# Taking turns at the start: two column groups of the first projection alternate, and the first loads are ordered anew

## The chip, the core and the metric

The kernel runs on one core of a Trainium2 chip. The core has five engines with programs of their own: TensorE (PE: matrix products and transposes into PSUM), VectorE (DVE), ScalarE (ACT), GpSimd (POOL) and SyncE (SP, which here only issues DMA transfers). SP, ACT and POOL can issue DMAs, each on a queue of its own. The metric is the time of one execution on the device, in microseconds (us).

## What is computed

One layer of a hybrid decoder trunk, on 256 prompt tokens and on 32 sample tokens (8 sequences of 4) at once, in float32:

```
proj = x @ w_in                                # 2048 -> 11280 columns
gB, gC, h, q, k, v, z, b, a, m_a, m_b = split(proj)
y_a = (gB * conv3(gC * h)) @ w_a_out           # histories of the sample: state_conv_a
q, k, v = split(silu(conv4([q, k, v])))        # histories of the sample: state_gdn_conv
y_b = gated_norm(delta_rule(l2norm(q), l2norm(k), v, g(a), sigmoid(b), S0), z) @ w_b_out
x = LN(ALPHA * x + (sigmoid(m_a) * y_a + sigmoid(m_b) * y_b) @ w_o)
x = LN(ALPHA * x + relu(x @ w_up)**2 @ w_down)
```

The results are the outputs for both sets of tokens and the new histories and states.

## The kernel before

**Stream.** All large products form one stream of 496 blocks. A block is 512 rows by 256 columns of a weight matrix (512 KB, four chunks of 128 rows); a column group of `w_in` is four blocks, which add into one accumulator in PSUM (`acc`, two buffers). Features lie on the partitions, tokens along the row, so x has to be there feature-major: `xh`, `xl`, 16 tiles of 288 tokens (256 prompt, 32 sample). Float32 products are made of three products of a faster type: x and weights are each split into a high part (a rounded copy, made by ACT) and a low part (the difference, made by DVE), and `matmuls(i)` issues, for each of 4 chunks and 2 column halves, high x high (L202), high x low (L203) and low x high (L204): 24 products of 288 columns a block.

**Order.** The schedule is written out by hand; each engine does its instructions in the order in which the program issues them. The loop over i does `split_hi(i + 3)` (L177), one step of the side work, `split_lo(i + 3)` (L140, a helper's line), the evacuations due at i, `matmuls(i)`, and `load(i + 7)` (L169, on SP). There are four buffers each for the raw weights, the high and the low part. `fill` is a list of small steps of which one is issued after every three products.

**Evacuation.** When a group of `w_in` is done, `conv_evac` takes its two halves out of PSUM in two steps one block apart (ACT copies with the histories in front, DVE does the width-4 convolution); a third step applies SiLU.

**Side work.** Gates and the delta rule (`gates`, `gdn`) are generators; one step is taken for every block from i = 4 on, and all must be over at block 112 (`mark["merge"]`).

**Start.** `warm` feeds 8 products into PSUM that are not used. SP then loads the identity (`cf`, first 128 columns), and in turn, four times: a quarter of x for the prompt (512 KB), a quarter for the sample (32 partitions), a weight block. POOL issues 16 transfers of histories and convolution weights (`hwr`, `har`). `x_tile(k)` turns one chunk of x: two transposes for the prompt (L736), one for the sample (L737), an ACT copy to `xh` and a DVE difference to `xl`. The first four chunks are turned ahead of block 0, the other twelve through `fill` in blocks 0 to 2. SP goes on with weight block 4, nine transfers of constants and small weights (L1263 to L1271), and blocks 5 and on. `hist_tiles` (L744 to L749) turns the histories at i = 4.

Of the kernel before, what the change touches and what calls it, by code (L numbers as in the profile page):

```python
# [9 lines left out]
F32 = mybir.dt.float32  # L10
F32R = mybir.dt.float32r
# [5 lines left out]
P = 128  # L17
D = 2048
NP_ = 256
NS = 32  # L20
NT = NP_ + NS
# [15 lines left out]

# [1 line left out]

# [64 lines left out]
def hybrid_kernel(ctx: ExitStack, tc: tile.TileContext, A):  # L104
# [15 lines left out]
    def nm(s):  # L120
        counter[0] += 1
        return f"{s}{counter[0]}"

    def gtile():
        n = nm("g")
        return gp.tile([P, 512], F32, tag="g", name=n)
# [12 lines left out]
    def tt(out, a, b, op):  # L139
        dve.tensor_tensor(out=out, in0=a, in1=b, op=op)  # L140
# [5 lines left out]

# [1 line left out]
    w_in = A["w_in"][0]  # L148
# [15 lines left out]
    def load(i):  # L164
        if i >= len(blocks):
            return
        gi, r0, k0, _, _ = blocks[i]
        t = wp.tile([P, KB, GW], F32, tag="raw", name=nm("raw"))
        sp.dma_start(t, gi["W"][r0:r0 + KB * P, gi["col0"]:gi["col0"] + GW]  # L169
                     .rearrange("(k p) c -> p k c", p=P))  # L170
        raw[i] = t

    def split_hi(i, step=KB):
        if i < len(blocks):
            his[i] = wp.tile([P, KB, GW], F32R, tag="hi", name=nm("hi"))
            for k in range(0, KB, step):
                act.copy(his[i][:, k:k + step], raw[i][:, k:k + step])  # L177
# [32 lines left out]

# [1 line left out]
    NE, NL = CF_AT["early"], CF_AT["late"]  # L212
# [30 lines left out]

# [1 line left out]
    gd = {}  # L245
# [3 lines left out]
    def conv_evac(sec, G, p):  # L249
# [37 lines left out]
        def last(ps):  # L287
            a1(ps)
            b1(ps)
        return [a0, b0, last]  # L290

    mark = {}
    for G in range(2):
        mark["kqv", G] = len(blocks)
        for sec, c0 in ((1, C_K), (0, C_Q), (2, C_V)):
            for p in range(2):
                add_group(w_in, c0 + 512 * G + GW * p, 0, KT, acts_x, conv_evac(sec, G, p))
        mark["kqv_end", G] = len(blocks)

    def h_evac(p):  # L300
# [319 lines left out]
    def final():  # L620
# [31 lines left out]

        # sample: four rows of the tile hold a token
        def moments():
# [46 lines left out]

# [1 line left out]
    tx_cm = tc.tile_pool(name="tx", bufs=1)  # L703
# [3 lines left out]
    wps = gtile()  # L707
    for _ in range(8):
        pe.matmul(wps, warm[:, 0:P], warm, start=True, stop=True)
    xr = [tx.tile([P, 3, 512], F32, name=f"xr{i}") for i in range(4)]  # L710
    xpr = A["x_prompt"][0].rearrange("(b p) f -> p b f", p=P)
    xsr = A["x_sample"].rearrange("b t f -> (b t) f")
    sp.dma_start(cf[:, 0:128], A["cf"][:, 0:128])
    for i in range(4):
        c = slice(512 * i, 512 * i + 512)
        sp.dma_start(xr[i][:, 0:2, :], xpr[:, :, c])
        sp.dma_start(xr[i][0:NS, 2, :], xsr[:, c])
        load(i)
    hwr = tx.tile([112, 768], F32, name="hwr")
    har = tx.tile([76, 256], F32, name="har")  # L720
    for g in range(4):
        c, c2 = slice(768 * g, 768 * g + 768), slice(256 * g, 256 * g + 256)
        gps.dma_start(hwr[28 * g:28 * g + 24, :], A["state_gdn_conv"][0].rearrange("b j c -> (b j) c")[:, c])
        gps.dma_start(hwr[28 * g + 24:28 * g + 28, :], A["gdn_conv_w"][0][:, c])
        gps.dma_start(har[19 * g:19 * g + 16, :], A["state_conv_a"][0].rearrange("b j c -> (b j) c")[:, c2])
        gps.dma_start(har[19 * g + 16:19 * g + 19, :], A["conv_a_w"][0][:, c2])
    lnr = tx.tile([33, P], F32, name="lnr")
    gps.memset(epsc[:, 0:1], LN_EPS)
    gps.memset(epsc[:, 1:2], NORM_EPS)
    gps.memset(epsc[:, 2:3], 1.28e-10)  # L730

    def x_tile(k):
        i, kk = k // 4, k % 4
        g = gtile()
        for b in range(2):
            pe.transpose(g[:, b * P:(b + 1) * P], xr[i][:, b, kk * P:(kk + 1) * P], ident)  # L736
        pe.transpose(g[:, NP_:NT], xr[i][0:NS, 2, kk * P:(kk + 1) * P], ident[0:NS, 0:NS])  # L737
        act.copy(xh[:, k, :], g[:, 0:NT])
        tt(xl[:, k, :], g[:, 0:NT], xh[:, k, :], SUB)

# [15 lines left out]

# [1 line left out]
    G_ = {}  # L758
# [90 lines left out]

# [1 line left out]
    def gdn(G):  # L851
# [126 lines left out]

        # sample: states times keys and queries, one sequence's columns at a time
        def states_of(hh):  # L980
# [8 lines left out]

        # inverse by doubling  # L990
        def pairs(out, a, b):
# [44 lines left out]
        def sample():  # L1036
            # sample: kernels of the short sequences
            sp1 = gtile()
# [101 lines left out]
        yield  # L1140
        # prompt: chunk by chunk
        S = T([P, 4, P], "E")
# [42 lines left out]
        while not done:  # L1185
            yield
        # gated norm (the norm of the queries folded in), to feature-major
        so = T([P, 9], "so")
# [28 lines left out]

# [1 line left out]
    def states():  # L1219
# [29 lines left out]

# [1 line left out]
    cur = [0]  # L1251
    aux = []
    his[0] = wp.tile([P, KB, GW], F32R, tag="hi", name=nm("hi"))
    los[0] = wp.tile([P, KB, GW], F32R, tag="lo", name=nm("lo"))
    t = raw.pop(0)
    for k in range(KB + 2):
        if k < KB:
            x_tile(k)
        if k > 1:
            act.copy(his[0][:, k - 2], t[:, k - 2])  # L1260
            tt(los[0][:, k - 2], t[:, k - 2], his[0][:, k - 2], SUB)
    load(4)
    sp.dma_start(cf[:, 128:], A["cf"][:, 128:NE])  # L1263
    sp.dma_start(cfe, A["cf"][:, NE:NL])
    sp.dma_start(ci, A["ci"])
    sp.dma_start(lnr[0:16, :], A["ln1_g"].rearrange("o (k p) -> (o k) p", p=P))
    sp.dma_start(lnr[16:32, :], A["ln1_b"].rearrange("o (k p) -> (o k) p", p=P))
    sp.dma_start(lnr[32:33, :], A["gdn_norm_w"])
    sp.dma_start(wbar, w_in[:, C_BA:C_BA + 16].rearrange("(k p) c -> p k c", p=P))
    sp.dma_start(arow[:, 0, :], A["a_log"].to_broadcast([P, 8]))  # L1270
    sp.dma_start(arow[:, 1, :], A["dt_bias"].to_broadcast([P, 8]))  # L1271
    for i in range(3):
        split_hi(i + 1, 2)
        split_lo(i + 1, 2)
        load(i + 5)
        fill.extend(lambda k=k: x_tile(k) for k in range(4 * i + 4, 4 * i + 8))
        matmuls(i)
    for i in range(4, AHEAD + 3):
        split_hi(i)
        split_lo(i)  # L1280
        load(i + 4)
    sgen = side()
    gcm = None
    for p in range(8):
        for n, f in enumerate(residual1(p)):
            at(mark["up"] + 6 + 4 * p + n, f)
    for i in range(3, len(blocks)):
        cur[0] = i
        split_hi(i + AHEAD)
        if i == 4:  # L1290
            hist_tiles()
            tx_cm.__exit__(None, None, None)
            gcm = tc.tile_pool(name="gdn", bufs=1)
            gpool = gcm.__enter__()
            gd["pool"] = gpool
            for G in range(2):
                gd["kq", G] = gpool.tile([P, 4, 4, 2, 64], F32, tag="kq", name=f"kq{G}", bufs=2)
                gd["kqs", G] = gpool.tile([P, 2, 4, 8, 4], F32, tag="kqs", name=f"kqs{G}", bufs=2)
                gd["v", G] = gpool.tile([P, 2, 4, 2, 64], F32, tag="vf", name=f"vf{G}")
                gd["vs", G] = gpool.tile([P, 4, 8, 4], F32, tag="vfs", name=f"vfs{G}")  # L1300
        if i > 3 and sgen:
            if i == mark["merge"]:
                for _ in sgen:
                    pass
                sgen = None
            else:
                next(sgen, None)
                if aux and next(aux[0], aux) is aux:
                    aux.pop(0)
            if i == mark["conv"] + 1:  # L1310
                gd["ao"] = ap_.tile([P, 2, H, NT], F32, tag="ao", name="ao")
# [25 lines left out]
        matmuls(i)  # L1337
        load(i + AHEAD + 4)
    for i in sorted(due):
        for f in due[i]:  # L1340
            f()
# [30 lines left out]
```

## Time and profile before

| | |
|---|---|
| time, median of 3 runs | 1725.30 us (1725.29 to 1725.32) |
| span of the profiled execution, first to last instruction | 1725.5 us |
| PE busy | 1701.8 us (99%) |
| DVE busy | 1026.3 us (59%) |
| ACT busy | 712.0 us (41%) |
| POOL busy | 123.7 us (7%) |
| DMA | 279.76 MB, 162 GB/s over the span |
| granted clock of TensorE, mean | 0.991 |

The profiled execution's time is its span; the times of the three runs were taken apart from it. A profile row of the timeline gives the start (us from the span's start), the duration, the engine, the line, the operation, output<-input, sizes, the number of instructions, and in brackets how long the engine had been idle and what ended that. A row of windows gives a stretch and the busy time of each engine in it (number of instructions in brackets), then the granted clock of TensorE (1.00 is full speed), the share of time in which the DMA engines were busy, and GB/s. SPq is SP's issuing of DMAs; a row of DMA issues gives the number, the size and the us from issue to landing.

### The profile page before, as it was taken

The page shows a single profiled execution, that of the slowest core. Times are in us where ns is not written, and L with a number is a line of the kernel's source. Part 1 is how long each engine was busy: PE and PEld are TensorE (multiplying, and loading weights), DVE is VectorE, ACT ScalarE, POOL GpSimd, SP SyncE. Part 2 cuts the span into 40 slices and gives each one's busy share as a digit, 9 for nine tenths or more (in the row PEclk, how much of TensorE's full clock was granted, in tenths as well). Part 3 has the DMA queues.
Part 4 walks back from the last instruction along what each step waited for, and adds up shares of the span by engine and source line. Part 5 has one row for each costly group of instructions (what it writes and reads, how often), then busy time and mean ns, then how long its engine had stood idle before and what let it go on. Part 6 is the DMA issues. An engine that isn't in the chain of part 4 may idle for free.

```text
span 1725.5 us, 31070 instructions
## 1 busy us (share of the span) xinstructions
PE 1701.8 (99%) x13037; PEld 1677.6 (97%) x13037; DVE 1026.3 (59%) x1345; ACT 712.0 (41%) x1031; POOL 123.7 (7%) x217
## 2 busy tenths in 40 slices
PE   9999999999999999999999999999999999999997
PEld 7999889999999999999999999999999999999996
DVE  5687777577454445545778754565445654456565
ACT  4664445334443333434445433344333433344331
POOL 2221231023300000000010000000000000000000
PEclk8999999999999999999999999999999999999998
DMA  8464347435655555555575555555555555555552
GB/s 241 141 181 137 106 118 233 131 103 151 207 169 162 169 165 166 159 171 160 170 204 164 166 168 163 168 160 167 166 167 163 159 171 166 165 164 166 163 158 78
DMA packets 272296, 279.76 MB, mean 162 GB/s; under 512 B 12122, under 2 KB 267035, under 8 KB 272023
## 3 DMA queue, kind: packets, MB, share of 16 engines
q1 hardware_dynamic: 267324, 265.87, 51.7%
q0 software_dynamic: 4256, 11.65, 2.3%
q8 instruction: 102, 1.67, 0.4%
q10 hardware_dynamic: 576, 0.26, 0.1%
q14 instruction: 38, 0.31, 0.0%
HBM read 270.26 MB, written 7.48 MB: 161 GB/s over the span
## 4 chain that ended last, share of the span: by engine, by line
issue 48%; PE 47%; DVE 2%; DMA 1%; ACT 1%; SPq 0%; POOLq 0%; POOL 0%; ACTq 0%; DVEq 0%
PE acc L202 14%; PE acc L203 14%; PE acc L204 14%; PE g L986 1%; DMA g<-in_ln_b_dram 1%; PE g L995 1%; DVE w L143 1%; DMA xr<-in_x_prompt_dram 0%; ACT hi L177 0%; DVE lo L140 0%; DVE w L266 0%; PE g L769 0%; DVE w L327 0%; PE g L1169 0%; PE g L1149 0%
## 5 line engine op out<-in xcount | busy, mean ns | idle before, releaser
L140 DVE TENSOR_TENSOR lo<-raw,hi 128x1024 fp32r<-128x1024 f32 (+2 forms) x502 | 608.0, 1214 | 551.6 <-ACT hi L177 549.1
L177 ACT CAST hi<-raw 128x1024 fp32r<-128x1024 f32 (+1 forms) x498 | 517.7, 1041 | 793.3 <-PE acc L203 729.7
L202 PE MATMUL acc<-xh,hi 128*128 128x288 f32 x1408 | 423.8, 301 | 0.0
L204 PE MATMUL acc<-xh,lo 128*128 128x288 f32 x1408 | 418.0, 297 | 0.0
L203 PE MATMUL acc<-xl,hi 128*128 128x288 f32 x1408 | 417.9, 297 | 0.0
L202 PE MATMUL acc<-dh,hi 128*128 128x290 f32 x1024 | 303.9, 297 | 0.0
L203 PE MATMUL acc<-dl,hi 128*128 128x290 f32 x1024 | 303.2, 296 | 0.0
L204 PE MATMUL acc<-dh,lo 128*128 128x290 f32 x1024 | 302.8, 296 | 0.0
L204 PE MATMUL acc<-hh,lo 128*128 128x288 f32 x1024 | 302.3, 295 | 0.0
L203 PE MATMUL acc<-hl,hi 128*128 128x288 f32 x1024 | 302.3, 295 | 0.0
L202 PE MATMUL acc<-hh,hi 128*128 128x288 f32 x1024 | 302.1, 295 | 0.0
L202 PEld LDWEIGHTS acc<-xh,hi 128*128 128x128 f32 x1408 | 266.8, 189 | 4.0 <-issue 1.6
L203 PEld LDWEIGHTS acc<-xl,hi 128*128 128x128 f32 x1408 | 266.9, 190 | 0.7
L204 PEld LDWEIGHTS acc<-xh,lo 128*128 128x128 f32 x1408 | 266.8, 189 | 0.0
L202 PEld LDWEIGHTS acc<-dh,hi 128*128 128x128 f32 x1024 | 193.6, 189 | 0.1
L204 PEld LDWEIGHTS acc<-dh,lo 128*128 128x128 f32 x1024 | 193.3, 189 | 0.0
L203 PEld LDWEIGHTS acc<-dl,hi 128*128 128x128 f32 x1024 | 193.2, 189 | 0.1
L203 PEld LDWEIGHTS acc<-hl,hi 128*128 128x128 f32 x1024 | 192.5, 188 | 0.0
L204 PEld LDWEIGHTS acc<-hh,lo 128*128 128x128 f32 x1024 | 192.3, 188 | 0.0
L202 PEld LDWEIGHTS acc<-hh,hi 128*128 128x128 f32 x1024 | 192.1, 188 | 0.0
L203 PE MATMUL acc<-ml,hi 128*128 128x288 f32 x256 | 75.6, 295 | 0.0
L204 PE MATMUL acc<-mh,lo 128*128 128x288 f32 x256 | 75.6, 295 | 0.0
(385 smaller groups left out, 1625.1 us busy)
## 6 DMA issues: line engine op xcount, KB each, us to landing
raw<-in_w_in_dram SPq DMA_DIRECT2D x176, 512.0 KB, 3.7
raw<-in_w_up_dram SPq DMA_DIRECT2D x128, 512.0 KB, 3.7
raw<-in_w_down_dram SPq DMA_DIRECT2D x128, 512.0 KB, 3.6
raw<-in_w_o_dram SPq DMA_DIRECT2D x32, 512.0 KB, 3.6
raw<-in_w_a_out_dram SPq DMA_DIRECT2D x16, 512.0 KB, 3.6
raw<-in_w_b_out_dram SPq DMA_DIRECT2D x16, 512.0 KB, 3.6
S<-in_state_gdn_dram POOLq DMA_DIRECT2D x8, 512.0 KB, 8.1
out_dram<-S POOLq DMA_DIRECT2D x8, 512.0 KB, 5.5
```

The lines of the kernel that those rows point to most:

```text
L140: dve.tensor_tensor(out=out, in0=a, in1=b, op=op)
L143: dve.scalar_tensor_tensor(out=out, in0=a, scalar=s, in1=b, op0=o0, op1=o1)
L177: act.copy(his[i][:, k:k + step], raw[i][:, k:k + step])
L202: pe.matmul(o, wh, xh_, start=st, stop=False)
L203: pe.matmul(o, wh, xl_, start=False, stop=False)
L204: pe.matmul(o, wl, xh_, start=False, stop=en)
L986: pe.matmul(o, kqm[:, 64 * b:64 * b + 64], S0[:, hh, b, :], start=(b == 0), stop=(b == 7))
L995: pe.matmul(out[r, q * 64:q * 64 + 64], a[r, q, :], b[r, q, :], start=True, stop=True)
```

## The change

- The first eight blocks, which were the four of column group 0 and then the four of group 1 (keys), are put in the order 0, 4, 1, 5, 2, 6, 3, 7: the two groups take turns, each chunk of x serving two blocks in a row. Group 0's two evacuation steps are made one (`pair`), since its accumulator has to be free when group 2 starts.
- x: the first quarter for the prompt comes in two halves and the sample in four transfers on ACT's queue; the other quarters stay on SP. The sample is packed: `xs4` holds 4 x 32 rows on 128 partitions, so one transpose turns four chunks. `x_steps(i)` turns four chunks in three steps (four transposes, one, four), with copies of two chunks or of the sample at a time. Chunks 1 to 3 (of four tiles each) are turned in blocks 1, 3 and 5.
- 18 instead of 8 unused products at the start.
- The histories are loaded on SP, not on POOL: `hist_loads()` stands between the first weight blocks (0 to 3) and blocks 4 to 6. The constants follow one by one after the loads of the loop at i = 2 to 5.
- `hist_tiles` moves from i = 4 to i = 6, and the side work begins at i = 10 instead of 4.

```diff
         def last(ps):
             a1(ps)
             b1(ps)
+        def pair(ps):
+            a0(ps)
+            b0(ps)
+        if G == 0 and sec == 1 and p == 0:
+            return [pair, last]
         return [a0, b0, last]
...
+    blocks[0:8] = [blocks[4 * (u % 2) + u // 2] for u in range(8)]
...
-    for _ in range(8):
+    for _ in range(18):
         pe.matmul(wps, warm[:, 0:P], warm, start=True, stop=True)
...
-    sp.dma_start(cf[:, 0:128], A["cf"][:, 0:128])
-    for i in range(4):
-        c = slice(512 * i, 512 * i + 512)
-        sp.dma_start(xr[i][:, 0:2, :], xpr[:, :, c])
-        sp.dma_start(xr[i][0:NS, 2, :], xsr[:, c])
-        load(i)
...
+    for u in range(2):
+        act.dma_start(xr[0][:, :, 256 * u:256 * u + 256], xpr[:, :, 256 * u:256 * u + 256])
+    for j in range(4):
+        act.dma_start(xs4[32 * j:32 * j + 32], xsr[:, :, j, :])
+    sp.dma_start(cf[:, 0:128], A["cf"][:, 0:128])
+    load(0)
+    load(1)
+    for i in range(1, 4):
+        sp.dma_start(xr[i], xpr[:, :, 512 * i:512 * i + 512])
+        if i == 1:
+            load(2)
+            load(3)
...
+    def hist_loads():
+        for g in range(4):
+            c, c2 = slice(768 * g, 768 * g + 768), slice(256 * g, 256 * g + 256)
+            sp.dma_start(hwr[28 * g:28 * g + 24, :], A["state_gdn_conv"][0].rearrange("b j c -> (b j) c")[:, c])
+            sp.dma_start(hwr[28 * g + 24:28 * g + 28, :], A["gdn_conv_w"][0][:, c])
+            sp.dma_start(har[19 * g:19 * g + 16, :], A["state_conv_a"][0].rearrange("b j c -> (b j) c")[:, c2])
+            sp.dma_start(har[19 * g + 16:19 * g + 19, :], A["conv_a_w"][0][:, c2])
+        sp.dma_start(lnr[0:16, :], A["ln1_g"].rearrange("o (k p) -> (o k) p", p=P))
+        sp.dma_start(lnr[16:32, :], A["ln1_b"].rearrange("o (k p) -> (o k) p", p=P))
+        sp.dma_start(lnr[32:33, :], A["gdn_norm_w"])
+
+    def x_steps(i):
+        def prompt(u):
+            g = gtile()
+            gv = g.rearrange("p (k t) -> p k t", k=2)
+            def turn(k, b):
+                c = (2 * u + k) * P
+                return lambda: pe.transpose(gv[:, k, b * P:(b + 1) * P], xr[i][:, b, c:c + P], ident)
+            def out():
+                ks = slice(4 * i + 2 * u, 4 * i + 2 * u + 2)
+                act.copy(xh[:, ks, 0:NP_], gv)
+                tt(xl[:, ks, 0:NP_], gv, xh[:, ks, 0:NP_], SUB)
+            return [turn(k, b) for k in range(2) for b in range(2)], out
...
+    for f in x_steps(0):
+        f()
+    split_hi(0, 2)
+    split_lo(0, 2)
+    hist_loads()
...
+    for i in range(1, AHEAD):
+        split_hi(i, 2)
+        split_lo(i, 2)
+    for i in range(4, AHEAD + 4):
+        load(i)
...
-    for i in range(3, len(blocks)):
+    for i in range(len(blocks)):
         cur[0] = i
         split_hi(i + AHEAD)
-        if i == 4:
+        if i in (1, 3, 5):
+            a_, b_, c_ = x_steps(i // 2 + 1)
+            idle = lambda: None
+            fill.extend([idle, idle, idle, a_, b_, idle, c_])
+        if i == 6:
             hist_tiles()
...
-        if i > 3 and sgen:
+        if i > 9 and sgen:
...
         matmuls(i)
         load(i + AHEAD + 4)
+        if 2 <= i < 6:
+            rest[i - 2]()
```

More of the change, by code (lines that the diff above doesn't have):

```diff
@@ L707, in hybrid_kernel @@
     wps = gtile()
-    for _ in range(8):
+    for _ in range(18):
         pe.matmul(wps, warm[:, 0:P], warm, start=True, stop=True)
-    xr = [tx.tile([P, 3, 512], F32, name=f"xr{i}") for i in range(4)]
+    xr = [tx.tile([P, 2, 512], F32, name=f"xr{i}") for i in range(4)]
+    xs4 = tx.tile([P, 4, P], F32, name="xs4")
     xpr = A["x_prompt"][0].rearrange("(b p) f -> p b f", p=P)
-    xsr = A["x_sample"].rearrange("b t f -> (b t) f")
-    sp.dma_start(cf[:, 0:128], A["cf"][:, 0:128])
-    for i in range(4):
-        c = slice(512 * i, 512 * i + 512)
-        sp.dma_start(xr[i][:, 0:2, :], xpr[:, :, c])
-        sp.dma_start(xr[i][0:NS, 2, :], xsr[:, c])
-        load(i)
+    xsr = A["x_sample"].rearrange("b t (i j f) -> (b t) i j f", j=4, f=P)
     hwr = tx.tile([112, 768], F32, name="hwr")
     har = tx.tile([76, 256], F32, name="har")
[L721 to L726, printed above, removed]
-    lnr = tx.tile([33, P], F32, name="lnr")
+    lnr = tx.tile([33, P], F32, name="lnr")
+    for u in range(2):
[10 more added lines that the diff above has]
+            load(3)
     gps.memset(epsc[:, 0:1], LN_EPS)
@@ L730, in hybrid_kernel @@
     gps.memset(epsc[:, 2:3], 1.28e-10)
[L732 to L739, printed above, removed]
+    def hist_loads():
[8 more added lines that the diff above has]
+        sp.dma_start(lnr[32:33, :], A["gdn_norm_w"])
@@ new lines, in x_steps, with sample, out, step @@
+    def x_steps(i):
+        def prompt(u):
+            g = gtile()
+            gv = g.rearrange("p (k t) -> p k t", k=2)
+            steps = []
+            def turn(k, b):
[6 more added lines that the diff above has]
+            return [turn(k, b) for k in range(2) for b in range(2)], out
+        def sample():
+            g = gtile()
+            gv = g[:, 0:P].rearrange("p (k t) -> p k t", k=4)
+            def out():
+                ks = slice(4 * i, 4 * i + 4)
+                act.copy(xh[:, ks, NP_:NT], gv)
+                tt(xl[:, ks, NP_:NT], gv, xh[:, ks, NP_:NT], SUB)
+            return [lambda: pe.transpose(g[:, 0:P], xs4[:, i, :], ident)], out
+        def step(part):
+            def f():
+                turns, out = part()
+                for g in turns:
+                    g()
+                out()
+            return f
+        return [step(lambda: prompt(0)), step(sample), step(lambda: prompt(1))]
@@ L1252, in hybrid_kernel @@
     aux = []
[L1253 to L1281, printed above, removed]
+    for f in x_steps(0):
[3 more added lines that the diff above has]
+    hist_loads()
+    rest = [lambda: sp.dma_start(cf[:, 128:], A["cf"][:, 128:NE]),
+            lambda: sp.dma_start(cfe, A["cf"][:, NE:NL]),
+            lambda: sp.dma_start(wbar, w_in[:, C_BA:C_BA + 16].rearrange("(k p) c -> p k c", p=P)),
+            lambda: (sp.dma_start(ci, A["ci"]),
+                     sp.dma_start(arow[:, 0, :], A["a_log"].to_broadcast([P, 8])),
+                     sp.dma_start(arow[:, 1, :], A["dt_bias"].to_broadcast([P, 8])))]
+    for i in range(1, AHEAD):
[3 more added lines that the diff above has]
+        load(i)
     sgen = side()
```

## The prediction

> **What bounds the kernel now.** I read the page first (busy time, clock), then the windows of 10 us for the stages that are not full, the order of TensorE (PE) and of SP's queue over the first 45 us, and last the DMA answers and the waits.
>
> ```profile
> PE 1701.8 (99%) x13037; PEld 1677.6 (97%) x13037; DVE 1026.3 (59%) x1345; ACT 712.0 (41%) x1031; POOL 123.7 (7%) x217
> 0.00:10.00 10.00, 6.69 (x22) 3.20 (x23) 2.00 (x6) 3.24 (x7) 5.97 (x16) 0.87 0.77 214
> 10.00:20.00 10.00, 9.39 (x36) 7.48 (x35) 5.57 (x12) 4.53 (x11) 2.67 (x8) 0.50 1.09 300
> 20.00:30.00 10.00, 10.00 (x63) 8.28 (x61) 4.50 (x9) 3.84 (x9) 0.00 (x0) 0.95 0.90 240
> 230.00:240.00 10.00, 8.25 (x37) 7.34 (x39) 7.44 (x15) 2.31 (x5) 3.48 (x2) 0.66 0.30 78
> ```
>
> PE is busy 99% of a span of 1725.5 us, so nothing on another engine matters unless PE waits for it. After the count in brackets of POOL, a window row gives the granted clock, the DMA share and GB/s: between 10 and 20 us PE is busy, but at clock 0.50. The change touches only the start and the blocks right behind it, so the question is when PE has finished a given block of the stream.
>
> ```profile
> 1.19 3.28 PE L709 MATMUL g<-warm 128*128 128x512 bf16 x8 [1.19 <-DVE warm L706]
> 9.44 0.61 PE L202 MATMUL acc<-xh,hi 128*128 128x288 f32 x1
> 17.71 0.44 PE L204 MATMUL acc<-xh,lo 128*128 128x288 f32 x1
> 22.44 0.40 PE L202 MATMUL acc<-xh,hi 128*128 128x288 f32 x1
> 22.95 0.38 PE L736 MATMUL g<-cf,xr 128*128 128x128 f32 x2
> 23.43 0.40 PE L202 MATMUL acc<-xh,hi 128*128 128x288 f32 x1
> 34.86 0.55 PE L744 MATMUL g<-cf,hwr 112*128 112x112 f32 x4
> 35.85 0.40 PE L202 MATMUL acc<-xh,hi 128*128 128x288 f32 x1
> 39.14 0.29 PE L202 MATMUL acc<-xh,hi 128*128 128x288 f32 x1
> 42.32 0.29 PE L202 MATMUL acc<-xh,hi 128*128 128x288 f32 x1
> 255.41 1.07 PE L1207 MATMUL g<-cf,xt 128*128 128x128 f32 x8
> ```
>
> The first product starts at 9.44. The rows at 39.14 and 42.32 start blocks 5 and 6: one block of 24 products takes 3.18 us at full clock, 0.133 us a product. The two L202 rows at 22.44 and 23.43 enclose three products and one x tile, 0.99 us, so a group of three transposes costs 0.59. The history transposes cost 35.85 - 34.86 = 0.99. Block 6 starts at 42.32 with the histories turned; the sum is made to this mark. Six blocks are 19.1 of it, the histories 1.0; the other 22 us is the start: 9.44 before the first product, 12 x 0.59 = 7.1 of transposes, the rest the low clock.
>
> **The change part by part: the loads.** [...]
>
> ```profile
> 6.64 0.42 SPq L169 DMA_DIRECT2D raw<-in_w_in_dram  x1
> 11.06 0.96 SPq L169 DMA_DIRECT2D raw<-in_w_in_dram  x2
> 13.36 1.46 SPq L1263 DMA_DIRECT2D cf<-in_cf_dram  x1
> 19.39 0.33 SPq L1267 DMA_DIRECT2D lnr<-in_ln_b_dram  x1
> 19.76 0.33 SPq L1268 DMA_DIRECT2D lnr<-in_gdn_norm_w_dram  x1
> 22.53 2.40 SPq L1270 DMA_DIRECT2D arow<-in_a_log_dram  x1
> 25.51 33.35 SPq L169 DMA_DIRECT2D raw<-in_w_in_dram  x12
> SPq L1263 <- DMA raw<-in_w_in_dram: 1.3, 1, 1.3
> SPq L1267 <- DMA xr<-in_x_prompt_dram: 1.3, 1, 1.3
> hwr<-in_state_gdn_conv_dram POOLq DMA_DIRECT2D x4, 72.0 KB, 6.3
> raw<-in_w_in_dram SPq DMA_DIRECT2D x176, 512.0 KB, 3.7
> raw<-in_w_in_dram SPq DMA_DIRECT2D x1, 512.0 KB, 4.4
> ```
>
> The two SPq waits (waiter, releaser, us in total) say that SP waits before a constant load for a weight block or for x, which that load does not read. [...] In the changed program the order on SP is: identity, weights 0 and 1, x quarter 1, weights 2 and 3, x quarters 2 and 3, **then 19 small transfers (16 for the histories, 3 for lnr), and only then weights 4 to 7**. [...]
>
> [...] Up to it 4416 KB are ordered (64 of identity, 512 and 256 of x and sample on ACT's queue, 2048 of weights, 1536 of x) and 203 KB of histories. Before, the load at 11.06 was released when 1664 KB had landed, and L1270 at 22.53 by weight block 4, at 4928 KB: 3264 KB in 11.47 us, 285 KB/us, beside most of the histories (412 KB, the 72 KB transfers the largest) on POOL's queue, some 290 KB, so 310. Counted on from 11.06 with about 120 KB of histories as landed, 4619 KB are there at 20.2. POOL's queue now stays empty, and rates reach more:
>
> ```profile
> 21.00:22.00 1.00, 1.00 (x8) 0.74 (x7) 0.00 (x1) 0.40 (x1) 0.00 (x0) 0.95 1.06 398
> ```
>
> At some 370 GB/s from 2.6 us on it would be 15.5. I take the middle, 17.8, since the sample's short rows speak for the slow end and the empty POOL queue for the fast one. Then 12 issues: 0.37 apart by the rows at 19.39 and 19.76, up to 0.55 by larger ones; I take 0.40, 4.8 us, issue at 22.6. The landing takes 4.4 by the first weight load after an idle queue (the first of the twelve at 25.51; the last row is that one), 3.7 by the median: 27.0.
>
> [...]
>
> **Who waits for block 4.** ACT runs in order, and the copies of x chunk 1 stand behind the high half of weight block 4 (split three blocks ahead); on DVE likewise the low half stands ahead of x chunk 1. Block 2 of the new order (first group, second chunk) needs that chunk.
>
> ```profile
> 34.93 1.05 ACT L177 CAST hi<-raw 128x1024 fp32r<-128x1024 f32 x1 [1.60 <-PE acc L203]
> 37.61 1.22 DVE L140 TENSOR_TENSOR lo<-raw,hi 128x1024 fp32r<-128x1024 f32 x1
> 14.02 0.69 DVE L140 TENSOR_TENSOR lo<-raw,hi 128x512 fp32r<-128x512 f32 x1 [2.59 <-ACT hi L177]
> 37.27 0.43 DVE L140 TENSOR_TENSOR wba<-ao,wba 128x256 fp32r<-128x256 f32 x1 [2.30 <-ACT wba L762]
> ```
>
> 27.0 + 1.05 + 1.22 + 0.69 for half a prompt chunk + 0.3 for the sample (128 columns, under 0.43) = 30.2: the second product of block 2. From both ends: 26.9 (15.5, 0.37, 3.7) to 34.6 (20.2, 0.55, 4.4).
>
> **From there to the mark.** Four blocks, 4 x 3.18 = 12.7. Two x chunks: four transposes cost the old group of three and one more, 0.59 + 0.13 (L1207, 1.07 for 8) = 0.72; a single one 0.59 - 0.26 = 0.33; 1.8 a chunk, 3.5. Histories 1.0. The clock: PE has stood still for about 10 us, and starts low. Two rows show how long:
>
> ```profile
> 232.00:233.00 1.00, 0.79 (x4) 0.51 (x4) 0.99 (x4) 0.03 (x1) 0.00 (x0) 0.86 0.00 0
> 239.00:240.00 1.00, 1.00 (x10) 0.75 (x10) 0.00 (x0) 0.46 (x1) 1.00 (x2) 0.73 0.84 227
> 233.62 0.61 PE L202 MATMUL acc<-xh,hi 128*128 128x288 f32 x1
> ```
>
> There dense work ran at half clock from 233.62 to about 239.5, 5.9 us, half of it lost: 2.9. At the start it ran so from 17.71 to about 21.05: 1.7. I take 2.3. Sum: 30.2 + 12.7 + 3.5 + 1.0 + 2.3 = 49.7, against 42.3: **7.4 us later** (3.5 to 12.6).
>
> **The other edits** lie inside that wait. Sample packing: one transpose a chunk instead of four, counted above. Eighteen warm products: 3.28 for the first 8, at most 8.6 us in all at the low clock, while x is on its way. x on ACT's queue spares SP issues of some 0.45 us. Taking turns needs one x chunk in two blocks instead of one each; that is its relief, and it goes unused while chunk 1 stands behind weight block 4. ACT's table load now follows its DMA issues, before x is turned. The constants go between weight loads of blocks 2 to 5, needed only from block 10. The evacuation of group 0 doubles up in block 7: DVE falls behind by about one block of work, with three blocks of lead; nothing on PE.
>
> **The side work** (gates, delta rule) starts at block 10 instead of 4; in PE's order every small step stands exactly one block later, and the last is over by block 102, ahead of the merge at 112, so nothing piles up there. Its alignment moves, and these waits may come out otherwise:
>
> ```profile
> PE g L1161 <- DVE v L143: 1.9, 2, 1.7
> PE g L1169 <- DVE v L140: 1.9, 1, 1.9
> PE g L1149 <- ACT E L1176: 1.6, 1, 1.6
> ```
>
> Zero for it, and 3 us either way: the 1.7 us wait at L1161 brought the low clock of 230 to 240 (0.66), which cost 2.9 and needn't come again; another 1.9 may bring one.
>
> **Total.** 1725.3 + 7.4 = 1732.7 (the profiled span, 1725.5, is 0.2 above the median of the runs, 1725.30, and the shift is taken over unchanged).
>
> **The rivals.** (1) *The forecast's stall, side work as before*: 1732.7, chance 0.55. (2) *The stall, but the low clock near 233 does not come again*: 1732.7 - 2.9 = 1729.8; for it, that a shift of some us suffices; with x's last quarter early, as low as 1726. Chance 0.22. (3) *The stall and a second low-clock stretch in the side work*: 1735.6, chance 0.12. (4) *The other side: weight block 4 comes in time.* It decides at 17: block 1 would end at 9.9 (first product, half a us after before, as the sample has to land first) + 6.4 + 1.8 + 1.7 (clock) = 19.8, and hi, lo and x need 3 us. Then the mark is at 19.8 + 17.2 = 37.0, 5.3 early: 1720.0. Against it: 4.6 MB by 17 less 9 us of issue and landing would need 8 us for what took 18. Chance 0.06. (5) *The change does not do what it says*: the histories are not in the way because their waits pass early, but x comes no earlier either; the wait is short, and the start ends about 3 us late, 1728.3. Chance 0.05.
>
> [...]
>
> **How the numbers follow.** The likeliest gives 1732.7; its own range is 1728.8 to 1737.9. With (2), (3) and the bounds, 1726.0 to 1738.0 leaves out (4) and the far ends. About 0.2%, 3.5 us, is what a measurement tells from no change: within it lie (5), the early part of (2) and a little of (1), 0.15; faster is (4) and a little of (2), 0.07; slower 0.78.
>
> **What would show it.** Right: ACT's high half of weight block 4 waits for a DMA landing at about 27; PE stands still from about 20 to 30 and then runs some us at clock 0.50; block 6 starts near 49.7. Wrong: weight block 4 landing before 20, or PE without a gap there. If the mark is right and the total is not, the side work moved: look at the waits of L1161, L1169, L1149's successors, and at the clock between 200 and 420 us.

## The result and the profile after

| | before | after |
|---|---|---|
| time, median | 1725.31 us (1725.29 to 1725.64, 4 runs) | 1739.11 us (1737.83 to 1740.3, 4 runs) |
| ratio, 95% interval | | 1.0081 [1.0069, 1.0093] |
| span of the profiled execution | 1725.5 us | 1736.9 us |
| granted clock, mean | 0.991 | 0.988 |
| start of block 6 | 42.32 us | 46.50 us |
| start of block 102 | 444.97 us | 455.55 us |

The change costs 13.8 us in the medians and 11.4 us between the two profiled executions. A run's time is its span plus 1.8 us in every run that has both, so the time of a profiled execution is not its span. The profiled execution of before would by that have taken 1725.5 + 1.8 = 1727.3 us, 2.0 more than the median; its mean clock is 0.991, where most other runs of this kernel have 0.992 to 0.995. The starts of blocks in this text are found by counting the rows of L202, L203 and L204 in PE's timeline, 24 products a block. "The mark" is the start of block 6.

First the wait that was forecast. SP's timeline of the changed kernel (start, duration, issue, number), around the first weight blocks:

```profile
15.69 0.32 SPq L745 DMA_DIRECT2D har<-in_state_conv_a_dram  x1
17.67 0.24 SPq L746 DMA_DIRECT2D har<-in_conv_a_w_dram  x1
18.02 0.30 SPq L743 DMA_DIRECT2D hwr<-in_state_gdn_conv_dram  x1
21.60 0.27 SPq L749 DMA_DIRECT2D lnr<-in_gdn_norm_w_dram  x1
21.98 8.88 SPq L169 DMA_DIRECT2D raw<-in_w_in_dram  x6
```

The eighth small transfer goes out at 17.67, after a pause of 1.7 us; the remaining ones follow 0.33 to 0.47 apart, and weight block 4 (the first of the six) goes out at 21.98. What hangs on it, in the chain of waits that ended last (start, duration, what) and in PE's timeline (in brackets: idle time before, and what ended it):

```profile
21.98 3.55 DMA raw<-in_w_in_dram
25.64 1.05 ACT hi L177
26.72 1.21 DVE lo L140
28.46 0.29 DVE xl L140
28.80 0.61 PE acc L203
```

```profile
11.24 0.33 PE L776 MATMUL g<-cf,xs 128*128 128x128 f32 x1 [3.16 <-DMA xs<-in_x_sample_dram]
13.20 0.61 PE L202 MATMUL acc<-xh,hi 128*128 128x288 f32 x1 [1.19 <-ACT hi L177]
27.39 0.61 PE L202 MATMUL acc<-xh,hi 128*128 128x288 f32 x1 [3.50 <-ACT xh L774]
28.80 0.61 PE L203 MATMUL acc<-xl,hi 128*128 128x288 f32 x1 [0.80 <-DVE xl L140]
46.50 0.40 PE L202 MATMUL acc<-xh,hi 128*128 128x288 f32 x1
```

The chain runs through every link that was named: landing, high half, low half, x's low part, second product of block 2. Block 6 starts at 46.50, 4.2 us later than before. So less than half of the 11.4 us lies in the start; 6.4 us arise between block 6 and block 102, where the side work is, and 0.8 behind. The windows (PE, PEld, DVE, ACT, POOL busy, then granted clock, DMA share, GB/s) and PE's waits (total, times, longest; the last two rows are of the kernel before) show where:

```profile
10.00:20.00 10.00, 7.57 (x33) 7.03 (x34) 5.73 (x9) 4.91 (x9) 0.00 (x0) 0.66 0.76 244
20.00:30.00 10.00, 5.70 (x38) 5.15 (x37) 3.28 (x5) 3.13 (x5) 0.00 (x0) 0.83 0.75 241
200.00:210.00 10.00, 6.66 (x43) 6.20 (x42) 9.43 (x14) 4.06 (x11) 3.47 (x7) 0.83 0.49 154
230.00:240.00 10.00, 9.95 (x76) 9.13 (x75) 9.66 (x19) 3.44 (x7) 4.82 (x2) 1.00 0.20 63
```

```profile
PE g L1215 <- DVE v L140: 3.3, 1, 3.3
PE g L1253 <- DVE xt L140: 2.9, 1, 2.9
PE g L1032 <- POOL b L1028: 2.7, 1, 2.7
PE g L961 <- ACT glx L956: 1.5, 1, 1.5
```

```profile
PE g L1207 <- DVE xt L140: 0.6, 1, 0.6
PE g L915 <- ACT glx L910: 0.5, 1, 0.5
```

The low clock of 230 to 240 (0.66 before) is gone, as in the second rival. In its place there are waits in other blocks: 200 to 210 has PE busy for 6.66 of 10 us, and DVE for 9.43. The lines of the delta rule have moved by 46: L1169 of before is L1215 now (1.9 then, 3.3 now), L1207 is L1253 (0.6 then, 2.9 now), L915 is L961 (0.5 then, 1.5 now).

### The profile page after: what moved, and what is told of

Read it like the earlier page. It is cut to its first block, busy times and chain, and to the rows that moved or that the text cites. A ratio compares the mean times of both kernels' runs of the same rounds, so it can differ in the third digit from the quotient of the medians.

```text
span 1736.9 us, 31050 instructions
## 1 busy us (share of the span) xinstructions
PE 1703.7 (98%) x13035; PEld 1681.2 (97%) x13035; DVE 1026.4 (59%) x1338; ACT 712.2 (41%) x1025; POOL 116.9 (7%) x201
## 4 chain that ended last, share of the span: by engine, by line
PE 91%; DVE 4%; issue 2%; DMA 1%; ACT 1%; POOL 1%; SPq 0%; ACTq 0%; DVEq 0%; POOLq 0%
PE acc L202 29%; PE acc L203 29%; PE acc L204 29%; PE g L1032 1%; DVE lo L140 1%; PE g L1041 1%; DVE w L143 1%; DMA raw<-in_w_in_dram 1%; DMA hwr<-in_state_gdn_conv_dram 0%; DVE w L334 0%; ACT b L1237 0%; ACT hi L177 0%; PE g L1195 0%; DMA out_dram<-S 0%; PE g L1215 0%
## 5 line engine op out<-in xcount | busy, mean ns | idle before, releaser
L140 DVE TENSOR_TENSOR lo<-raw,hi 128x1024 fp32r<-128x1024 f32 (+1 forms) x499 | 607.7, 1220 | 567.7 <-ACT hi L177 565.3
L202 PE MATMUL acc<-xh,hi 128*128 128x288 f32 x1408 | 424.9, 302 | 4.7 <-ACT xh L774 3.5
L203 PE MATMUL acc<-xl,hi 128*128 128x288 f32 x1408 | 419.3, 298 | 0.8 <-DVE xl L140 0.8
L204 PE MATMUL acc<-xh,lo 128*128 128x288 f32 x1408 | 419.4, 298 | 0.0
L202 PE MATMUL acc<-dh,hi 128*128 128x290 f32 x1024 | 303.9, 297 | 0.0
L203 PE MATMUL acc<-dl,hi 128*128 128x290 f32 x1024 | 303.2, 296 | 0.0
L204 PE MATMUL acc<-dh,lo 128*128 128x290 f32 x1024 | 302.7, 296 | 0.0
L204 PE MATMUL acc<-hh,lo 128*128 128x288 f32 x1024 | 302.3, 295 | 0.0
L203 PE MATMUL acc<-hl,hi 128*128 128x288 f32 x1024 | 302.3, 295 | 0.0
L202 PE MATMUL acc<-hh,hi 128*128 128x288 f32 x1024 | 302.1, 295 | 0.0
L202 PEld LDWEIGHTS acc<-xh,hi 128*128 128x128 f32 x1408 | 268.8, 191 | 8.6 <-ACT xh L774 3.7
L203 PEld LDWEIGHTS acc<-xl,hi 128*128 128x128 f32 x1408 | 268.5, 191 | 1.9 <-DVE xl L140 1.1
L204 PEld LDWEIGHTS acc<-xh,lo 128*128 128x128 f32 x1408 | 267.9, 190 | 0.3 <-DVE lo L140 0.3
L202 PEld LDWEIGHTS acc<-dh,hi 128*128 128x128 f32 x1024 | 193.6, 189 | 0.1
L204 PEld LDWEIGHTS acc<-dh,lo 128*128 128x128 f32 x1024 | 193.3, 189 | 0.0
L203 PEld LDWEIGHTS acc<-dl,hi 128*128 128x128 f32 x1024 | 193.2, 189 | 0.1
L203 PEld LDWEIGHTS acc<-hl,hi 128*128 128x128 f32 x1024 | 192.5, 188 | 0.0
L204 PEld LDWEIGHTS acc<-hh,lo 128*128 128x128 f32 x1024 | 192.3, 188 | 0.0
L202 PEld LDWEIGHTS acc<-hh,hi 128*128 128x128 f32 x1024 | 192.1, 188 | 0.0
L203 PE MATMUL acc<-ml,hi 128*128 128x288 f32 x256 | 75.6, 295 | 0.0
L204 PE MATMUL acc<-mh,lo 128*128 128x288 f32 x256 | 75.6, 295 | 0.0
```

What stands on the lines that cost most here:

```text
L202: pe.matmul(o, wh, xh_, start=st, stop=False)
L203: pe.matmul(o, wh, xl_, start=False, stop=False)
L204: pe.matmul(o, wl, xh_, start=False, stop=en)
```

## The experiments

The theory after the result: (a) the 19 small transfers ahead of weight block 4 cost about 7 us; (b) the rest comes from the side work, by the shift of the delta rule by one block or by the gates, which now fill blocks 10 to 20: eleven steps, the last of them directly ahead of the delta rule, which therefore starts at 21. Before, they filled blocks 4 to 14, and the delta rule waited for block 20. All kernels were run next to the kernel before; ratios are to it.

**The histories behind weight blocks 4 to 6.**

```diff
-    hist_loads()
...
     for i in range(4, AHEAD + 4):
         load(i)
+    hist_loads()
```

> The changed kernel with the 19 history transfers moved behind weight blocks 4 to 6 on SP's queue, nothing else. Theory (the wait for weight block 4 sets the start): the gap before block 2 (27.39 start, 3.5 + 0.8 us of waiting, then a block at the low clock) goes, block 6 starts near 39.6 instead of 46.5, the total falls by about 7 us from 1739.1 to about 1732, and the side work stays as in the changed kernel. Rival (bandwidth at the start sets it, whatever the order): weight block 4 still lands after 24 us, block 6 stays after 45, the total within 2 us of 1739.

1731.16 us (1729.82 to 1731.72, 6 runs), ratio 1.0032 [1.002, 1.0043]: 8.0 us less than the changed kernel. SP's and PE's timelines:

```profile
15.05 2.77 SPq L169 DMA_DIRECT2D raw<-in_w_in_dram  x3
17.88 0.51 SPq L743 DMA_DIRECT2D hwr<-in_state_gdn_conv_dram  x1
23.91 0.29 PE L202 MATMUL acc<-xh,hi 128*128 128x288 f32 x1
39.60 0.40 PE L202 MATMUL acc<-xh,hi 128*128 128x288 f32 x1
```

Weight block 4 goes out 6.9 us earlier, block 2 starts without a wait, and block 6 starts at 39.60 instead of 46.50, 2.7 us ahead of the kernel before. Yet the kernel is slower than before by 5.9 us: part (a) is shown, and what is left lies behind the mark, where (b) would have to be.

**x on SP's queue instead of ACT's.** The changed kernel with the first quarter of x and the four sample transfers issued by SP.

```diff
-        act.dma_start(xr[0][:, :, 256 * u:256 * u + 256], xpr[:, :, 256 * u:256 * u + 256])
+        sp.dma_start(xr[0][:, :, 256 * u:256 * u + 256], xpr[:, :, 256 * u:256 * u + 256])
...
-        act.dma_start(xs4[32 * j:32 * j + 32], xsr[:, :, j, :])
+        sp.dma_start(xs4[32 * j:32 * j + 32], xsr[:, :, j, :])
```

> The changed kernel with the six transfers of x's first quarter and the sample on SP's queue, ahead of the identity, instead of ACT's. Theory: they are hidden behind weight block 4, block 6 stays at 46 to 48 and the span within 2 us of 1736.9; if the 1.8 us by which the time exceeds the span in the changed kernel come of ACT's queue, the time falls to about 1737 at the same span. Rival (a queue of its own brings x earlier and that counts): the first product moves from 13.2 to 15 or later and the total grows by the same 2 us or more.

1737.33 us (1736.9 to 1739.32, 4 runs), ratio 1.0071 [1.0056, 1.0086]. PE's timeline:

```profile
9.38 0.40 PE L202 MATMUL acc<-xh,hi 128*128 128x288 f32 x1 [1.47 <-ACT hi L177]
28.65 0.61 PE L202 MATMUL acc<-xh,hi 128*128 128x288 f32 x1 [9.64 <-ACT xh L774]
```

The first product comes at 9.38, not 13.20: with x and the sample on ACT's queue, beside the identity and two weight blocks on SP's, the sample lands late (its transpose waits 3.16 us for it); ahead of them on one queue the first product comes 3.8 us sooner. Nothing of this reaches the mark (48.03): weight block 4 goes out at 23.36, and PE only waits longer behind it, 9.64 us instead of 3.50. The relief is real and lies in front of a later wait. The span is 1.6 us shorter (1735.3) although the mark is 1.5 later; where that comes from is told with the table below.

**The delta rule alone one block later, in the kernel before.**

```diff
-            while cur[0] < mark["kqv", G] + 20 or aux:
+            while cur[0] < mark["kqv", G] + 21 or aux:
```

> The kernel before with nothing changed but the delta rule held back by one block (it waits for block 21 instead of 20). Theory: the same waits as in the changed kernel appear at blocks 24 to 25, 44, 69 and 96 and the low clock at block 51 goes; total 1725.3 + 6.3 = about 1731.6. [...]

1728.78 us (1727.45 to 1730.07, 10 runs), ratio 1.0019 [1.001, 1.0029], +3.5 us, about half of what was expected. PE's waits:

```profile
PE g L1169 <- DVE v L140: 3.3, 1, 3.3
PE g L1207 <- DVE xt L140: 2.9, 1, 2.9
PE g L986 <- POOL b L982: 2.7, 1, 2.7
```

These are the three waits of the changed kernel (L1215, L1253 and L1032 there), to a tenth, in a kernel whose start is that of before. The fourth, at L961, is not among them.

**The side work from block 9 instead of 10, and from block 7.** With both the delta rule starts at block 20 again, as before; from block 9 the gates still end right ahead of it (at 19), from block 7 two blocks lie in between (five before).

```diff
-        if i > 9 and sgen:
+        if i > 8 and sgen:     # first run
+        if i > 6 and sgen:     # second run
```

> The changed kernel with the side work starting at block 9 instead of 10, so that the delta rule stands at the same blocks as in the kernel before. Theory (the shift by one block against the evacuations makes new waits): the waits before L961, L1215, L1032 and L1253 (1.5, 3.3, 2.7, 2.9 us) and the low clock behind them go, the old ones (blocks 43, 51) come back, the total falls by about 6 us to about 1733. [...]

> The changed kernel with the side work starting at block 7 instead of 10: the gates end at block 17, three blocks ahead of the delta rule, which starts at block 20 as in the kernel before. Theory (the gates' last step right ahead of the delta rule makes the wait before L961): blocks 23 to 24 take 4.95 + 3.19 us as in the kernel before (5.89 + 4.72 in the changed one one block later, 10.16 + 4.86 with the start at block 9), the other blocks as in the kernel before; total 1739.1 - 3.8 (gates) - 1.9 (shift) = about 1733.4. Rival (the place of the delta rule alone decides): the wait stays, total about 1737 as with the start at block 9.

From block 9: 1737.26 us (1737.18 to 1738.61, 4 runs), ratio 1.0068 [1.0051, 1.0085], a miss: 1.9 us gained, far from what was expected. From block 7: 1729.86 us (1729.26 to 1732.26, 5 runs), ratio 1.0032 [1.0019, 1.0045], 9.3 us gained. PE's timeline of the run from block 9:

```profile
120.07 1.52 PE L961 MATMUL g<-glx,hmr 128*128 128x512 f32 x2 [5.49 <-ACT glx L956]
```

The three shift waits are back to their old sizes in both (L1215 1.9, L1253 0.6, L1032 at most 0.4). With the gates adjacent, the wait at L961 grew to 5.5 us instead. ACT's timeline shows what is in the way there, first in the changed kernel, then in the kernel before:

```profile
109.25 1.28 ACT L276 ACT_TABLE_LOAD   x1
112.90 1.03 ACT L177 CAST hi<-raw 128x1024 fp32r<-128x1024 f32 x1
115.41 1.03 ACT L177 CAST hi<-raw 128x1024 fp32r<-128x1024 f32 x1
116.34 0.62 ACT L956 CAST glx<-gl 128x512 fp32r<-128x512 f32 x1
```

```profile
106.15 0.41 ACT L276 ACTIVATE vf<-w 128x256 f32<-128x256 f32 x1
107.95 0.61 ACT L910 CAST glx<-gl 128x512 fp32r<-128x512 f32 x1
```

In the changed kernel a table load of 1.28 us stands ahead of the SiLU of the values (L276, 109.25), where the kernel before has none (106.15); on ACT the gates' exponential (L865, 100.14) comes between it and the last SiLU (L281, 96.40). The steps behind it, down to `glx`, come late (116.34 against 107.95). In the run from block 7 this load is gone again, together with the wait at L961; that the load is the largest part of the delay was not tested.

**Gates early, delta rule one block late**, to separate the two: `i > 6` and `mark["kqv", G] + 21` in the changed kernel, three blocks between gates and delta rule.

> The changed kernel with the gates three blocks earlier (side work from block 7 on) and the delta rule one block later than in the run with early gates alone, so exactly where the changed kernel has it. Theory: gates and shift add. The gates' part goes (block 24 near 3.2 instead of 4.72, no wait of 1.5 us at L961), the shift's part stays: blocks 43, 68 and 95 near 9.2, 8.4 and 8.2, blocks 51 and 52 near 4.4 and 4.8. Median 1729.9 + 3.5 = 1733.4. Rival: the shift only costs where the gates stand right ahead of it: 1730. Second rival: gates cost nothing by themselves and all of the 9.3 us is the shift: 1739.

1732.91 us (1731.97 to 1734.69, 5 runs), ratio 1.0044 [1.003, 1.0058]. In the medians the gates are worth 6.2 us (1739.11 to 1732.91), the shift 3.05 (1732.91 to 1729.86; the last two intervals overlap, but the +3.5 in the kernel before says the same). The two do not simply add: with the gates adjacent, taking the shift away gained only 1.9. PE's waits of this kernel, with the three of the shift and none at L961:

```profile
PE g L1215 <- DVE v L140: 3.3, 1, 3.3
PE acc L202 <- ACT xh L774: 3.3, 1, 3.3
PE g L1253 <- DVE xt L140: 2.9, 1, 2.9
PE g L1032 <- POOL b L1028: 2.7, 1, 2.7
```

Block by block, in us from PE's timelines (blocks numbered as before; with the delta rule shifted, the block one later; "early gates" and "no turns" are runs with the side work from block 7, the latter told below; "x on SP" has the side work of after):

| block | 23 | 24 | 42 | 43 | 50 | 51 | 67 | 68 | 94 | 95 | sum |
|---|---|---|---|---|---|---|---|---|---|---|---|
| before | 4.95 | 3.19 | 6.65 | 6.18 | 7.25 | 7.45 | 5.17 | 3.29 | 5.04 | 3.52 | 52.7 |
| early gates | 3.74 | 3.18 | 6.64 | 6.18 | 7.58 | 6.99 | 5.16 | 3.29 | 5.04 | 3.52 | 51.3 |
| no turns | 3.64 | 3.18 | 7.00 | 5.83 | 6.95 | 4.81 | 5.17 | 3.29 | 5.04 | 3.52 | 48.4 |
| gates early, shift | 3.64 | 3.17 | 8.97 | 4.98 | 4.38 | 4.82 | 7.93 | 3.30 | 7.40 | 3.52 | 52.1 |
| before, shift | 3.64 | 3.18 | 9.22 | 5.70 | 4.38 | 4.82 | 7.95 | 3.30 | 8.44 | 3.91 | 54.5 |
| from block 9 | 10.16 | 4.86 | 7.00 | 5.82 | 6.96 | 4.82 | 5.16 | 3.29 | 5.04 | 3.52 | 56.6 |
| x on SP | 5.88 | 4.71 | 9.02 | 4.95 | 4.37 | 4.82 | 7.95 | 3.30 | 7.40 | 3.52 | 55.9 |
| after | 5.89 | 4.72 | 9.23 | 4.71 | 4.38 | 4.80 | 8.40 | 4.37 | 8.22 | 4.30 | 59.0 |

The ten blocks hold 59.0 - 52.7 = 6.3 of the 6.4 us between the mark and block 102. Blocks 23 and 24 are the gates' place, 42, 67 and 94 the shift's (against the run without turns, in which block 51 takes 4.81 us, against 4.80 in after with the clock at 1.00 there: +3.7 net, after 2.6 given back in block 50). Of the 6.9 us by which after exceeds the run with gates early and shift, 3.8 lie in blocks 23 and 24 and 3.1 in 67, 68, 94 and 95, where the clock of after fell to 0.50.

These 3.1 us are not the gates': the run with x on SP has the same side work at the same blocks and does not have them (7.95, 3.30, 7.40, 3.52), which is why its span is the shorter. Windows of 3.41 us around the wait in block 67, first of after, then of x on SP, show the difference:

```profile
306.45:309.86 3.41, 1.36 (x13) 1.36 (x13) 3.27 (x9) 0.28 (x1) 1.76 (x4) 1.00 0.65 194
309.86:313.28 3.42, 3.42 (x16) 3.09 (x15) 1.05 (x2) 1.03 (x3) 1.21 (x1) 0.50 0.33 113
```

```profile
308.35:311.76 3.41, 1.72 (x16) 1.72 (x16) 3.30 (x8) 0.00 (x0) 1.63 (x4) 1.00 0.77 233
311.76:315.17 3.41, 3.41 (x27) 3.24 (x25) 0.69 (x2) 1.03 (x3) 1.88 (x5) 1.00 0.23 80
```

Between 40 and 1720 us the clock of after is low (0.50) four times, for 3.41 us each, from 118.71, 204.04, 309.86 and 432.74. In these rows, 3.41 us with PE busy for 1.36 were followed by the low clock, 3.41 us with 1.72 were not; whether that decides is not shown. So 3.8 us of the gates' price are located, and how much of the remaining difference of the medians is theirs stays open.

**Both repairs**: histories behind weight blocks 4 to 6, side work from block 7.

> Both repairs: the histories behind weight blocks 4 to 6, and the side work from block 7 on. Theory: they add, 1739.1 - 8.0 - 5.7 = about 1725.4, no difference from the kernel before: what is left of the change's gain at the start (block 6 at 39.6 instead of 42.3) is about 2.7 us less what else. [...]

1722.42 us (1721.76 to 1723.11, 10 runs), ratio 0.9984 [0.9975, 0.9993]: faster than the kernel before by 2.5 us against the runs beside it (1724.96), by 2.9 against the first ones (1725.31). Taken one after the other, the steps are gates 6.2, shift 3.05, histories 7.4 (1729.86 to 1722.42), and -2.9 for the rest of the change, 13.8 together; a chain of differences sums up in any case, and only the two prices of the histories (8.0 and 7.4) and of the shift (3.5 and 3.05) were taken twice.

**All of x on SP, in the order of need** (each quarter behind the weight block that is split before it), with both repairs:

```diff
+    sp.dma_start(cf[:, 0:128], A["cf"][:, 0:128])
     for u in range(2):
-        act.dma_start(xr[0][:, :, 256 * u:256 * u + 256], xpr[:, :, 256 * u:256 * u + 256])
+        sp.dma_start(xr[0][:, :, 256 * u:256 * u + 256], xpr[:, :, 256 * u:256 * u + 256])
...
     for i in range(4, AHEAD + 4):
         load(i)
+        if i < 6:
+            sp.dma_start(xr[i - 2], xpr[:, :, 512 * (i - 2):512 * (i - 2) + 512])
+    hist_loads()
```

> Both repairs, and in addition all of x on SP's queue in the order identity, x quarter 0, sample, weights 0 and 1, x quarter 1, weights 2, 3 and 4, x quarter 2, weights 5, x quarter 3, weights 6, histories. Theory (the sample's transfers beside weight blocks 0 and 1 on the other queue hold the first product back to 13.2): the first product at about 9.4, no gap before block 2, block 6 near 34.5, total about 5 us below both repairs alone, about 1720.5: faster than the kernel before. Rival (the DMA engines cannot bring weight block 4 and x any earlier, so the gap comes back at block 2): block 6 not before 38, total 1724 or more.

1721.18 us (1719.71 to 1722.08, 10 runs), ratio 0.9977 [0.9968, 0.9987]; the mark is at 36.94, not 34.5: the first product comes at 10.11, and waits for x follow (0.48 and 1.01 us at block 2, 0.67 ahead of the history transposes). From both repairs alone (1722.42) this differs by 1.2 us, with ranges that overlap.

**Eighteen warm products in the kernel before**, nothing else (`range(8)` to `range(18)`).

> The kernel before with 18 unused products at the start instead of 8, nothing else. Theory: the clock stays full up to about 10.9 instead of 7.5, which covers the first transposes and a product or two; block 1 starts up to 1 us earlier, the total is 0 to 1 us lower, not to be told from 1725.3. Rival (a longer warm-up keeps the clock up through the whole start): block 1 starts 4 us earlier and the total falls to about 1721.

1721.44 us (1720.87 to 1724.98, 10 runs), ratio 0.9982 [0.9973, 0.9991]. The edit that the prediction costed at nothing gains 3.5 us in the kernel before, as much as all the repaired kernels. Windows of 2 us, first of this kernel, then of the kernel before:

```profile
10.00:12.00 2.00, 1.50 (x8) 1.11 (x9) 1.28 (x4) 0.61 (x3) 1.65 (x4) 0.99 1.09 305
18.00:20.00 2.00, 2.00 (x13) 1.79 (x12) 1.29 (x2) 1.03 (x3) 0.00 (x0) 0.80 1.10 335
```

```profile
10.00:12.00 2.00, 1.40 (x6) 0.72 (x4) 1.43 (x4) 0.86 (x3) 1.96 (x4) 0.50 1.13 343
18.00:20.00 2.00, 2.00 (x10) 2.00 (x10) 1.35 (x3) 0.89 (x2) 0.00 (x0) 0.50 1.09 323
```

With 18 the clock is still up between 10 and 12, where it was down before, and it is up again before 20. This trace does not show the whole gain: its execution (1724.98) was the slowest of the ten, and block 6 starts at 40.69, 1.6 us earlier than in the trace of before; the kernel with the shifted delta rule, whose start is that of before, has 41.13. Where the rest of the 3.5 us lies is not shown.

**Eight warm products in the ordered start.**

> The kernel with all of x on SP in the order of need (median 1721.18, clock 1.00 from 4 to 22 us, block 6 at 36.94), with 8 unused products at the start instead of 18. Theory: the 10 more warm products are what keeps the clock up at the start, as in the kernel before with 18 of them (3.5 us); with 8 the clock falls to 0.50 for at least one stretch before 20 us, block 6 comes near 40, median 1724.7. Rival: here PE's work at the start is dense enough by itself (first product at 10.11, no wait in block 1), the clock stays up or falls for under 2 us, 1721 to 1722.

1720.96 us (1719.21 to 1721.7, 9 runs), ratio 0.9974 [0.9965, 0.9984]: no loss, the theory fell. The clock does fall, as the window of this kernel (first) beside that with 18 shows:

```profile
12.00:14.00 2.00, 2.00 (x11) 2.00 (x10) 0.36 (x1) 0.00 (x0) 0.00 (x0) 0.50 1.08 383
12.00:14.00 2.00, 2.00 (x17) 2.00 (x17) 0.80 (x2) 0.00 (x0) 0.00 (x0) 1.00 1.09 380
```

Block 3 starts at 23.47 with 8 and at 23.45 with 18. In this start block 2 waits for x anyway (0.48 and 1.01 us with 18, 0.49 with 8), and a slow clock ahead of it mostly fills those waits. In the kernel before PE is busy for 9.39 of the 10 us up to 20, with little idle time to fill.

**Without taking turns**, on the kernel with both repairs: blocks 0 to 7 in the old order, x turned in blocks 0 to 2, histories in block 4, and group 0's two evacuation steps apart again (`pair` is gone; not shown).

```diff
-    blocks[0:8] = [blocks[4 * (u % 2) + u // 2] for u in range(8)]
...
-        if i in (1, 3, 5):
-            a_, b_, c_ = x_steps(i // 2 + 1)
+        if i in (0, 1, 2):
+            a_, b_, c_ = x_steps(i + 1)
...
-        if i == 6:
+        if i == 4:
             hist_tiles()
```

> The kernel with the histories behind weight blocks 4 to 6 and the early gates (median 1722.42), without taking turns: blocks 0 to 3 are group 0 again, x chunks 1 to 3 are turned in blocks 0 to 2, the histories in block 4. Theory: taking turns hides a wait for weight block 3, which ACT splits at 19.11 to 20.16 ahead of x chunk 1; without it block 1 needs that chunk at about 18 and gets it at about 21.5, a gap of 3.5 us, block 6 at about 41.7 instead of 38.20, median 1726. Rival: the order of the blocks is worth nothing, since x is there by 17.7 either way: 1722.4, block 6 at 38. Second rival: the gap also drops the clock for a stretch: 1727.5.

1722.24 us (1721.7 to 1722.96, 11 runs), ratio 0.9981 [0.9972, 0.999]: the same as with turns, so the change's main idea brings nothing to the total here. The expectation misread a row: what ACT splits at 19.11 is weight block 4, and without turns x chunk 1 does not stand behind it. Block 6 starts 1.9 us later (40.12), 0.7 of it from a first product at 13.90 instead of 13.18; block 51 (4.81 against 6.34 with turns) gives 1.5 of that back.

## Why the prediction was right in its direction and wrong in its size

The forecast was 1732.7 (1726.0 to 1738.0); the median is 1739.11, 6.4 us above it and 1.1 above the range.

- **The loads: right.** The forecast lets the eighth small transfer wait for the landing of x's last quarter (17.8), with 12 issues from there to weight block 4 (22.6); no run ahead of the result shows that it has to. The changed kernel shows the wait itself: SP stands 1.7 us for `xr` (L746) and issues at 17.67, weight block 4 goes out 12 issues later, at 21.98. It lands at 25.5 (27.0): 0.6 from the earlier issue, the rest because the landing took 3.55 us, nearer to the median row (3.7) than to the one that was taken (4.4).
- **Who waits for it: right.** The second product of block 2 starts at 28.80 (30.2), the whole difference being the earlier landing. Undoing the order gave 8.0 us back, 7.4 in the kernel with early gates, against a forecast of 7.4 for the start as a whole.
- **From there to the mark: too much.** 46.50 - 28.80 = 17.7 us against 19.5. A chunk of x costs 0.98 (block 3, 4.17, less 3.19), not 1.8: the old group of three (0.59) and one more was no measure for nine transposes in three groups. With histories (0.99) and two chunks, 2.0 is left for the low clock (2.3). The mark moved by 4.2 us, not 7.4, inside its bounds of 3.5 to 12.6 (the upper one adds up to 12.3 from its own terms: 34.5, not 34.6, + 12.7 + 3.5 + 1.0 + 2.9 - 42.3).
- **First product: missed.** 13.20, where rival (4) put it at 9.9, half a us after before. The transpose of the sample waits 3.16 us for its transfer. In the changed kernel it costs nothing, as it lies ahead of the longer wait.
- **The other edits: half right.** Taking turns brings nothing to the total, as was said, and not when weight block 4 is early either. The warm products were costed at nothing. In the ordered start they are nothing (1720.96 with 8, 1721.18 with 18), yet they are worth 3.5 us in the kernel before; to ask whether PE's low clock (0.50 from 7.44 to 21.09) lies on the path could have told, as PE was busy for 9.39 of the 10 us from 10 on.
- **The side work: the step that failed.** "Zero for it, and 3 us either way". It was +6.4 between the traces up to block 102 (9.25 in the medians: 6.2 for the gates, 3.05 for the shift), and 3.1 of the 6.4 are a low clock that another run with the same side work did not have. The shift was seen and set to zero, with no row that said so: against the evacuations the wait at L1169 went from 1.9 to 3.3 us, that at L1207 from 0.6 to 2.9, and one of 2.7 came new. The gates were not seen at all: that "every small step stands exactly one block later" holds for the delta rule, while the gates moved by six blocks, and the five idle blocks between the two were gone. Blocks 23 and 24 alone took 3.8 us more by it than with the gates early. The text followed the last step of the side work and not the distance between its parts.
- **Total.** The span was compared with the median of the times, although a time is the span plus 1.8 us: the profiled execution was 2.0 us above the median, not 0.2. The forecast of rival (2), that the clock near 233 does not fall again, came true in the changed kernel (1.00 from 230 to 240), and the loss came on top. With the measured terms: 1725.3 + 4.2 to the mark + 6.4 up to block 102 + 0.8 behind it + 2.0 for the untypical trace of before + 0.4 for the changed kernel's own trace (its time, 1738.71, is below its median) gives 1739.1.
- **Runs and clock.** The three runs ahead of the prediction lay within 0.03 us. More runs differ: the kernel before 1724.09 to 1728.86 over all studies, with 18 warm products 1720.87 to 1724.98. The mean clock of the runs of before lies between 0.990 and 0.995; the slowest, 1728.86, has 0.990, the fastest, 1724.09, has 0.992. How much of the differences is the clock's is not shown.

## What to carry to other kernels

When side work is moved along a main stream, ask for each of its parts both how far it moved against the stream's own periodic work and how far against its neighbours; a generator that starts later and still ends in time can lose the slack inside. On a shared issue queue, whatever is needed first goes first, and many small transfers go behind the last load that is on the path, even when each takes 0.3 us to issue. Before a gain is expected from better order, look for the next wait behind it: a first product 3.8 us earlier, and a clock of 0.50 instead of 1.00 between 12 and 14 us, moved nothing where the weight block or x was late anyway. And before a difference between two traces is put down to an edit, look for a third trace with the same work: here it took 3.1 us away from the gates.

## What the runs showed that was not expected

A wait on PE had two prices here: the wait itself, and a low clock behind it in some executions and not in others (behind the wait at L1032, which is 2.7 us in after, 0.50 there against 1.00 with x on SP). The same side work gave the same block times to some hundredths of a us in two kernels with starts 7 us apart (8.40 and 4.37 in after, 8.43 and 4.33 with the histories behind), which looks like a pattern in the order of the work. The run with x on SP, with the same order of work, has 7.95 and 3.30, so that order alone does not make it. What else decides whether the clock falls behind the wait is not shown.
